# Whole expert groups in three fp32r products instead of full float32 ones: a mixture-of-experts kernel on one Trainium2 core

## The chip, the core and the metric

The kernel runs on one core of one Trainium2 chip. The metric is the device time of one execution in microseconds, as the median of repeated runs. TensorE (PE) multiplies, VectorE (DVE), ScalarE (ACT) and GpSimd (POOL) do the rest, and SyncE (SP) issues the loads of weights.

## The reference, cut to what matters

Two layers over 256 latent tokens (and 256 context tokens that only the first mixer reads), width 1024. Each layer is a token mixer followed by a mixture of experts; a final norm ends it. What matters here is the mixture:

```
def swiglu(x, w_gu, w_down):
    g, u = jnp.split(x @ w_gu, 2, axis=-1)
    return (jax.nn.silu(g) * u) @ w_down
...
    def expert_block(args):
        tok, w, e = args
        return swiglu(x_pad[tok], w_gu[e], w_down[e]) * w[:, None]
...
    return routed + swiglu(xn, ws_gu, ws_down)
```

There are 64 experts of inner width 256; each token goes to 8 of them, and one shared expert sees all. An expert's weights are three tiles of 1 MB: two of gate and up (128 x 2048 floats each, four chunks of 512 columns), one of down.

## The kernel before

**Experts by rank.** The router's counts sort the experts. The five largest, two natural ones and the shared one are *dense*: they run over all 256 tokens, with weights split into a high part (a cast to fp32r, `wh`) and a low part (the rest, `wl`), three products a step (`mm3`). The other experts get 32 to 128 slots each. Four units of 32 slots make a *group* of 128 rows; two groups make a batch, 11 batches a layer. In batches 0, 5 and 9 the first group (groups 0, 10 and 18) holds one expert with all 128 slots; the other groups hold two to four experts side by side, each on its own columns of the PE array. All groups multiply in full float32.

**A batch.** `first(i)`: gate and up of group i in two halves of four steps (`gate_up`), the transposed slot matrix (`slot_side`), and for i = 0 the scatter of the batch before. `second(i)`: transpose of the inner values (`flip`, tile `ht`), half of the next batch's `gather` of tokens (tile `xg`), then `down`, which writes `Y` with ScalarE (high part) and VectorE (low part). At a batch's start GpSimd builds the slot matrix `S` of the next batch. Ahead of batch 0 stands a branch, `overflow`, that all engines pass.

**Order.** Every engine runs its instructions in the recorded order. A planner at build time (`Stream`, `until`, `COST`) guesses when each load lands and puts steps of dense experts (`up`) where a group's tiles would not be there yet. Loads go through a ring of twelve 1 MB tiles (`wr`, `wx`); SP issues one as soon as a tile is free.

**The splitter.** `splitter(tmp, tiles, eng, bufs)` makes high and low parts of one 512-column chunk at a time, two chunks ahead of the one asked for, out of one pool of `wh` and `wl` buffers that all splitters share:

```
            while len(out) < min(q + 3, last or 4 * len(tiles)):
...
                S.copy(out=hi, in_=t)
                eng(i, c).tensor_tensor(out=lo, in0=t, in1=hi.bitcast(F32), op=OP.subtract)
```

`lower` gives even chunks to GpSimd, odd ones to VectorE. In the functions below, L309 is the matmul helper, L566 and L567 the two parts of a chunk, L1407 the build of S, L1473 and L1475 the copies of gathered tokens, L1535 the copy of `ht`, L1548 and L1549 the two parts of Y.

Of the kernel before, what the change touches and what calls it, by code (L numbers as in the profile page):

```python
# [10 lines left out]
F32 = mybir.dt.float32  # L11
# [83 lines left out]
RK, GROUPS = make_plan()  # L95
NG = len(GROUPS)


# [133 lines left out]
ORDER = 4.0  # L232
COST = dict(step=1.46, down2=2.95, half=3.6, side=0.6, scatter=4.0, flip=0.25, gather=2.0, down=3.6)

# [69 lines left out]
def _body(nc, tc, a, pp, rp, ps, ps1, dr):  # L304
# [846 lines left out]
    def moe(l, tail):  # L1151
      rsb = bank()
      with tc.tile_pool(name=f"e{l}", bufs=1) as mp, tc.tile_pool(name=f"e{l}t", bufs=2) as tp:
# [36 lines left out]
        def over_all(ns, gate=None, eng=None, early=None):  # L1190

            wq = splitter(tp, ns, eng or lower, 5)
            if early is not None:
# [34 lines left out]
        def all_down(f, n):  # L1228

            f, at = f  # L1230
            wq = splitter(tp, [n], lower, 5)

# [229 lines left out]
        def gather(b, half):  # L1462
# [3 lines left out]
            for d2 in range(2 * half, 2 * half + 2):  # L1466
# [4 lines left out]
                o = xg[:, 2 * d2:2 * d2 + 2, :].rearrange("p a s -> p (a s)")  # L1471
                if d2 % 2:
                    S.copy(out=o, in_=p)  # L1473
                else:
                    V.tensor_copy(out=o, in_=p)  # L1475
# [30 lines left out]
        gu = {}  # L1506

        def gate_up(g, ks=range(8)):
            xg = xgs[g // 2]
            b0 = (g % 2) * P  # L1510
# [4 lines left out]
            for k in ks:  # L1515
                for q, j, o, wd in rr:
                    mm(p[o:o + wd, :], xg[:, k, b0 + o:b0 + o + wd], st.tile(wt[q][k // 4])[:, 512 * (k % 4):512 * (k % 4) + 512], k == 0, k == 7)
                if k % 4 == 3:
                    for q in sorted({u[0] for u in GROUPS[g]}):
                        if last_use[q] == g:  # L1520
                            st.free(wt[q][k // 4])
            if 7 not in ks:
                return
            h = tp.tile([P, 256], F32, name="h", bufs=2)
# [4 lines left out]
        def flip(g):  # L1529
            h = hts[g]  # L1530
            p = bank()
            for k in range(2):
                PE.transpose(p[:, k * P:(k + 1) * P], h[:, k * P:(k + 1) * P], ident)  # L1533
            o = tp.tile([P, 2, P], F32, name="ht", bufs=2)
            S.copy(out=o, in_=p[:, :256].rearrange("p (k s) -> p k s", k=2))  # L1535
            hts[g] = o

        def down(g):
# [3 lines left out]
            for c in range(2):  # L1542
                p = bank()
                for k in range(2):
                    for q, j, o, wd in rr:
# [6 lines left out]
            for q in sorted({u[0] for u in GROUPS[g]}):  # L1552
                if last_use[q] == g:
                    st.free(wt[q][2])
# [35 lines left out]
        for b in range(NB):  # L1590
# [6 lines left out]
            def first(i):  # L1597
                g = 2 * b + i
                qs = sorted({u[0] for u in GROUPS[g]})
                for part in range(2):  # L1600
                    until([wt[q][part] for q in qs])
                    gate_up(g, range(4 * part, 4 * part + 4))
                    spend("half")
                slot_side(g)
# [5 lines left out]
            def second(i):  # L1610
# [6 lines left out]
                down(g)  # L1617
                spend("down")

            for step in (first, second) if b + 1 < NB else ():  # L1620
                for i in range(2):
                    step(i)
# [56 lines left out]
```

## Time and profile before

| | us |
|---|---|
| median of 3 runs | 1469.41 (1467.08 to 1471.1) |
| the profiled execution | 1469.6 |
| its span, first to last instruction | 1467.7 |
| TensorE busy (matmuls) | 1392.4, 95% of the span |
| VectorE, ScalarE, GpSimd busy | 753.6, 518.7, 331.8 |

The page gives busy shares over the whole span. The kernel has stages with different limits: the first mixer to about 250 us, mixture 0 to about 770 us, the second mixer to about 950 us, mixture 1 to the end. A busy share in a stage comes from the windows view, and what ends an engine's idle time from the waits and the timeline.

### The profile page before, as it was taken

Reading aid. Unit: us, or ns where it says so; the run is one execution under the profiler, and the core shown is the slowest. Engines: PE = TensorE matmul, PEld = TensorE weight load, DVE = VectorE, ACT = ScalarE, POOL = GpSimd, SP = SyncE. Lnnn points to the kernel's source line nnn. Section 1 sums busy time; section 2 is a strip of 40 time slices with the busy share of each in tenths; the row PEclk is TensorE's granted clock in tenths of the full one; section 3 lists DMA queues with packets and bytes.
Section 4 is the critical chain, followed back from the end, with each engine's and each line's share of the span. In section 5 each row is a group of like instructions: output and inputs, shape, how many; then the busy total and the mean of one; then the engine's idle time right before and its main releaser. Section 6 shows DMA issues by size and latency. Waiting matters only on the chain. (4 is left out here: it accounts for less than half of the span.)

```text
span 1467.7 us, 27203 instructions
## 1 busy us (share of the span) xinstructions
PE 1392.4 (95%) x10752; PEld 973.3 (66%) x10752; DVE 753.6 (51%) x1375; ACT 518.7 (35%) x874; POOL 331.8 (23%) x415
## 2 busy tenths in 40 slices
PE   6999997899999999999999999899999999999997
PEld 4677776656566575666657899775656666566664
DVE  6789997524343333334346786542334334343534
ACT  4777882422122222222225445432212222212222
POOL 1300044421222112312001451431212212111210
PEclk9999999899999999999999999999999999999999
DMA  9876694589989999999999744369999999999994
GB/s 376 321 276 245 245 375 186 222 351 409 412 362 405 420 420 420 420 418 421 420 418 388 289 163 173 116 251 412 394 389 372 421 421 421 420 419 420 420 420 182
DMA packets 77443, 514.85 MB, mean 351 GB/s; under 512 B 9856, under 2 KB 10240, under 8 KB 17024
## 3 DMA queue, kind: packets, MB, share of 16 engines
q1 hardware_dynamic: 74720, 508.91, 85.3%
q10 hardware_dynamic: 2592, 4.16, 0.9%
q8 instruction: 86, 1.41, 0.4%
q14 instruction: 45, 0.37, 0.1%
HBM read 511.99 MB, written 1.05 MB: 350 GB/s over the span
## 5 line engine op out<-in xcount | busy, mean ns | idle before, releaser
L309 PE MATMUL b<-wr,xg 128*32 128x512 f32 (+2 forms) x1464 | 306.5, 600 | 4.6 <-DMA wr<-in_m_gu 2.9
L567 POOL TENSOR_TENSOR wl<-wr,wh 128x512 fp32r<-128x512 f32 (+1 forms) x82 | 121.2, 1492 | 704.5 <-ACT wh L566 654.5
L309 PE MATMUL b<-wx,xg 128*32 128x512 f32 (+2 forms) x744 | 234.3, 598 | 1.7 <-SPq L1430 1.4
L566 ACT CAST wh<-wr 128x512 fp32r<-128x512 f32 (+1 forms) x230 | 147.4, 682 | 84.5 <-PE b L309 44.8
L567 DVE TENSOR_TENSOR wl<-wr,wh 128x512 fp32r<-128x512 f32 (+1 forms) x148 | 145.4, 1010 | 57.6 <-ACT wh L566 57.4
L309 PEld LDWEIGHTS b<-wr,xg 128*32 128x32 f32 (+2 forms) x1464 | 83.9, 118 | 134.9 <-issue 119.5
L1159 DVE SCALAR_TENSOR_TENSOR xT<-b,mod,xT 128x256 f32<-128x256 f32 x304 | 130.0, 478 | 60.5 <-PE b L309 54.5
L309 PE MATMUL s<-hh,wh 128*128 128x256 f32 x512 | 152.3, 297 | 1.1 <-ACT wh L566 1.1
L309 PE MATMUL s<-hh,wl 128*128 128x256 f32 x512 | 145.5, 284 | 3.7 <-DVE wl L567 1.9
L1526 DVE TENSOR_TENSOR h<-h,b 128x256 f32<-128x256 f32 x44 | 18.5, 420 | 252.4 <-ACT h L1525 252.4
L309 PE MATMUL s<-hl,wh 128*128 128x256 f32 x512 | 144.7, 283 | 0.0
L309 PE MATMUL b<-wr,ht 128*32 128x512 f32 (+2 forms) x712 | 141.9, 596 | 1.5 <-ACT ht L1535 1.5
L1549 DVE SCALAR_TENSOR_TENSOR Y<-b,gt,Y 128x512 fp32r<-128x512 f32 x88 | 65.8, 750 | 150.8 <-ACT Y L1548 150.8
L1525 ACT ACTIVATE h<-b 128x256 f32<-128x256 f32 x44 | 16.9, 384 | 351.0 <-PE b L309 351.0
L309 PEld LDWEIGHTS s<-hh,wh 128*128 128x128 f32 x512 | 98.2, 192 | 28.7 <-issue 25.3
L309 PE MATMUL b<-wx,ht 128*32 128x512 f32 (+2 forms) x392 | 109.1, 595 | 0.5 <-ACT ht L1535 0.5
L1548 ACT ACTIVATE Y<-b,gt 128x512 fp32r<-128x512 f32 x88 | 60.3, 687 | 135.8 <-PE b L309 129.5
L309 PEld LDWEIGHTS s<-hh,wl 128*128 128x128 f32 x512 | 98.1, 192 | 4.8 <-DVE wl L567 2.5
L1407 POOL TENSOR_SCALAR S<-cst,agq 128x32 fp32r<-128x32 f32 (+3 forms) x208 | 83.2, 429 | 72.2 <-PE b L309 54.5
L567 POOL TENSOR_TENSOR wl<-wx,wh 128x512 fp32r<-128x512 f32 (+1 forms) x36 | 53.6, 1506 | 199.2 <-ACT wh L566 192.6
L309 PEld LDWEIGHTS s<-hl,wh 128*128 128x128 f32 x512 | 98.3, 192 | 0.4
L309 PE MATMUL b<-S,xt 128*128 128x256 f32 x704 | 94.5, 287 | 0.0
(283 smaller groups left out, 2744.3 us busy)
## 6 DMA issues: line engine op xcount, KB each, us to landing
wr<-in_m_gu SPq DMA_DIRECT2D x167, 1024.0 KB, 12.7
wx<-in_m_gu SPq DMA_DIRECT2D x89, 1024.0 KB, 12.8
wr<-in_m_dn SPq DMA_DIRECT2D x80, 1024.0 KB, 11.1
wx<-in_m_dn SPq DMA_DIRECT2D x42, 1024.0 KB, 11.4
wr<-in_ada_w SPq DMA_DIRECT2D x32, 1024.0 KB, 9.1
wr<-in_a_in SPq DMA_DIRECT2D x10, 1024.0 KB, 8.1
wr<-in_ada SPq DMA_DIRECT2D x8, 1024.0 KB, 12.2
wr<-in_b_out SPq DMA_DIRECT2D x6, 1024.0 KB, 7.2
```

Of the source, the lines that this page charges most:

```text
L309: PE.matmul(out, lhsT, rhs, start=start, stop=stop, skip_group_check=True)
L566: S.copy(out=hi, in_=t)
L567: eng(i, c).tensor_tensor(out=lo, in0=t, in1=hi.bitcast(F32), op=OP.subtract)
L1159: V.scalar_tensor_tensor(out=xT[:, d, :], in0=y, scalar=mod[:, l, 5, d:d + 1], in1=xT[:, d, :], op0=OP.mult, op1=OP.add)
L1407: (G if b else V).tensor_scalar(out=s[:, tt, i * P + o:i * P + o + wd], in0=C["iota1"][:, j:j + wd], scalar1=agq[:, tt, q:q + 1], scalar2= ...
L1525: S.activation(out=h, in_=p[:, :256], func=AF.Silu)
L1526: V.tensor_tensor(out=h, in0=h, in1=p[:, 256:], op=OP.mult)
L1548: S.activation(out=hi, in_=p, func=AF.Copy, scale=gts[g])
L1549: V.scalar_tensor_tensor(out=y[:, 1, 512 * c:512 * c + 512], in0=p, scalar=gts[g], in1=hi.bitcast(F32), op0=OP.mult, op1=OP.subtract)
```

## The change

For the three groups a layer that hold one expert alone (`WHOLE`), gate, up and down run as three fp32r products a step on high and low parts, instead of one full float32 product. The gathered tokens of such a group are written as two parts (`xh`, `xl`) straight out of `gather`, the inner values as two parts (`h4`) out of `flip`, and the weights go through a splitter of their own: `begin` opens it, and asks for the first two chunks if the planner thinks that the tile has landed; for gate and up that is at the start of the batch, for down in `flip`. All splitters' pools have four buffers instead of five, and the planner's cost of a half of gate and up, and of down, is 2.8 instead of 3.6 for these groups.

```diff
--- before.py
+++ after.py
@@ -94,6 +94,9 @@
 
 RK, GROUPS = make_plan()
 NG = len(GROUPS)
+
+WHOLE = [len({q for q, _ in g}) == 1 for g in GROUPS]
+assert not any(WHOLE[1::2])
 
 
 def batch_tiles():
@@ -230,7 +233,7 @@
 LOAD, LATE = 2.6, -0.3
 
 ORDER = 4.0
-COST = dict(step=1.46, down2=2.95, half=3.6, side=0.6, scatter=4.0, flip=0.25, gather=2.0, down=3.6)
+COST = dict(whole=2.8, step=1.46, down2=2.95, half=3.6, side=0.6, scatter=4.0, flip=0.25, gather=2.0, down=3.6)
 
 READY = 5.0
 
@@ -1189,7 +1192,7 @@
 
         def over_all(ns, gate=None, eng=None, early=None):
 
-            wq = splitter(tp, ns, eng or lower, 5)
+            wq = splitter(tp, ns, eng or lower, 4)
             if early is not None:
                 early.append(wq)
             p, out, at = [], [], []
@@ -1228,7 +1231,7 @@
         def all_down(f, n):
 
             f, at = f
-            wq = splitter(tp, [n], lower, 5)
+            wq = splitter(tp, [n], lower, 4)
 
             def step(c):
                 pb2 = [bank(), bank()]
@@ -1469,7 +1472,15 @@
                     for n in range(4):
                         mm(p[:, 256 * i:256 * i + 256], xt[:, n // 2, n % 2, (2 * d2 + i) * P:(2 * d2 + i + 1) * P], s[:, n % 2, :], n == 0, n == 3)
                 o = xg[:, 2 * d2:2 * d2 + 2, :].rearrange("p a s -> p (a s)")
-                if d2 % 2:
+                if WHOLE[2 * b]:
+                    if d2 == 0:
+                        xls[b] = [tp.tile([P, 8, P], F32R, name=n, bufs=1) for n in ("xh", "xl")]
+                    o, pv = xg[:, 2 * d2:2 * d2 + 2, :], p.rearrange("p (a s) -> p a s", a=2)
+                    hi, lo = (x[:, 2 * d2:2 * d2 + 2, :] for x in xls[b])
+                    S.copy(out=hi, in_=pv[:, :, :P])
+                    V.tensor_copy(out=o[:, :, P:], in_=pv[:, :, P:])
+                    V.tensor_tensor(out=lo, in0=pv[:, :, :P], in1=hi.bitcast(F32), op=OP.subtract)
+                elif d2 % 2:
                     S.copy(out=o, in_=p)
                 else:
                     V.tensor_copy(out=o, in_=p)
@@ -1505,7 +1516,33 @@
 
         gu = {}
 
+        xls, wsp = {}, {}
+
+        def there(n):
+            return st.arrival(n) <= st.now
+
+        def begin(g, part):
+
+            q = GROUPS[g][0][0]
+            if WHOLE[g] and (g, part) not in wsp:
+                ns = wt[q][:2] if part == 0 else wt[q][2:]
+                wsp[g, part] = splitter(tp, ns, lower, 4)
+                if there(ns[0]):
+                    wsp[g, part](-1)
+
         def gate_up(g, ks=range(8)):
+            if WHOLE[g]:
+                xh, xl = xls[g // 2]
+                if 0 in ks:
+                    gu[g] = bank()
+                    begin(g, 0)
+                t1 = wt[GROUPS[g][0][0]][1]
+                for k in ks:
+                    w_ = wsp[g, 0](k, None if k > 3 or there(t1) else 4)
+                    mm3(gu[g], xh[:, k, :], xl[:, k, :], *w_, k == 0, k == 7)
+                if 7 in ks:
+                    hidden(g, gu[g])
+                return
             xg = xgs[g // 2]
             b0 = (g % 2) * P
             if 0 in ks:
@@ -1519,8 +1556,10 @@
                     for q in sorted({u[0] for u in GROUPS[g]}):
                         if last_use[q] == g:
                             st.free(wt[q][k // 4])
-            if 7 not in ks:
-                return
+            if 7 in ks:
+                hidden(g, p)
+
+        def hidden(g, p):
             h = tp.tile([P, 256], F32, name="h", bufs=2)
             S.activation(out=h, in_=p[:, :256], func=AF.Silu)
             V.tensor_tensor(out=h, in0=h, in1=p[:, 256:], op=OP.mult)
@@ -1531,8 +1570,16 @@
             p = bank()
             for k in range(2):
                 PE.transpose(p[:, k * P:(k + 1) * P], h[:, k * P:(k + 1) * P], ident)
+            pv = p[:, :256].rearrange("p (k s) -> p k s", k=2)
+            if WHOLE[g]:
+                o = tp.tile([P, 2, 2, P], F32R, name="h4", bufs=1)
+                S.copy(out=o[:, 0], in_=pv)
+                V.tensor_tensor(out=o[:, 1], in0=pv, in1=o[:, 0].bitcast(F32), op=OP.subtract)
+                hts[g] = o
+                begin(g, 1)
+                return
             o = tp.tile([P, 2, P], F32, name="ht", bufs=2)
-            S.copy(out=o, in_=p[:, :256].rearrange("p (k s) -> p k s", k=2))
+            S.copy(out=o, in_=pv)
             hts[g] = o
 
         def down(g):
@@ -1541,7 +1588,10 @@
             y = tp.tile([P, 2, D], F32R, name="Y", bufs=2)
             for c in range(2):
                 p = bank()
-                for k in range(2):
+                if WHOLE[g]:
+                    for k in range(2):
+                        mm3(p, o_[:, 0, k], o_[:, 1, k], *wsp[g, 1](2 * c + k), k == 0, k == 1)
+                for k in () if WHOLE[g] else range(2):
                     for q, j, o, wd in rr:
                         mm(p[o:o + wd, :], o_[:, k, o:o + wd], st.tile(wt[q][2])[:, 1024 * c + 512 * k:1024 * c + 512 * k + 512], k == 0, k == 1)
                 hi = y[:, 0, 512 * c:512 * c + 512]
@@ -1550,7 +1600,7 @@
                                        op0=OP.mult, op1=OP.subtract)
             ys[g] = y
             for q in sorted({u[0] for u in GROUPS[g]}):
-                if last_use[q] == g:
+                if last_use[q] == g and not WHOLE[g]:
                     st.free(wt[q][2])
 
         def scatter(b, tl=None):
@@ -1600,7 +1650,7 @@
                 for part in range(2):
                     until([wt[q][part] for q in qs])
                     gate_up(g, range(4 * part, 4 * part + 4))
-                    spend("half")
+                    spend("whole" if WHOLE[g] else "half")
                 slot_side(g)
                 spend("side")
                 if i == 0 and b:
@@ -1615,8 +1665,9 @@
                     spend("gather")
                 until([wt[q][2] for q in sorted({u[0] for u in GROUPS[g]})])
                 down(g)
-                spend("down")
-
+                spend("whole" if WHOLE[g] else "down")
+
+            begin(2 * b, 0)
             for step in (first, second) if b + 1 < NB else ():
                 for i in range(2):
                     step(i)
```

What it does to the order is seen in two places. ScalarE at the seam between batch 4 and batch 5 of layer 0 (Y of group 9, then group 10), before, with what each instruction waits for in brackets (the engine whose counter it watches; DMAHW is a landing):

```order
L1548 ACTIVATE Y_5056<-b_5057,gt_4874 128x512 [waits DVE_49,PE_49]
L1548 ACTIVATE Y_5056<-b_5064,gt_4874 128x512 [waits PE_49]
L1535 COPY ht_5096<-b_5093 128x256 [waits PE_49]
L1473 COPY xg_5035<-b_5108 128x512 [waits PE_49]
L566 CAST wh_5118<-wx1_4083 128x512 [waits Pool_49]
L1548 ACTIVATE Y_5145<-b_5146,gt_5028 128x512 [waits DVE_49,PE_49]
L1548 ACTIVATE Y_5145<-b_5157,gt_5028 128x512 [waits PE_49]
L1525 ACTIVATE h_5207<-b_5194 128x256 [waits PE_49]
L566 CAST wh_5263<-wx0_4172 128x512 [waits DMAHW3_49,Activation_49]
```

and now:

```order
L1582 COPY ht_5260<-b_5257 128x256 [waits PE_49]
L1480 CAST xh_5203<-b_5262 128x256 [waits PE_49]
L1480 CAST xh_5203<-b_5274 128x256 [waits PE_49]
L569 CAST wh_5286<-wx2_4255 128x512 [waits Activation_49]
L1598 ACTIVATE Y_5313<-b_5314,gt_5186 128x512 [waits DVE_49,PE_49]
L1598 ACTIVATE Y_5313<-b_5325,gt_5186 128x512 [waits PE_49]
L569 CAST wh_5353<-wr2_5076 128x512 [waits DMAHW2_49,Pool_49]
L569 CAST wh_5357<-wr2_5076 128x512 [waits Activation_49]
L569 CAST wh_5362<-wr2_5076 128x512 [waits PE_49,Pool_49]
L569 CAST wh_5369<-wr2_5076 128x512 [waits DVE_49,PE_49]
L569 CAST wh_5384<-wr4_5087 128x512 [waits DMAHW3_49,PE_49,Pool_49]
L569 CAST wh_5388<-wr4_5087 128x512 [waits DVE_49,PE_49]
```

The casts of group 10's gate and up chunks (six of the eight are shown) now stand between the last Y copy of group 9 and the activation `h` of group 10; from the third on they also wait for TensorE, whose earlier chunks hold the buffers.

GpSimd at the start of batch 0 of layer 0, behind the branch (S of batch 1, then low parts `wl`), before:

```order
L1407 TENSOR_SCALAR S_2846<-cst_71,agq_2559 128x64 [waits DVE_49]
L1407 TENSOR_SCALAR S_2846<-cst_71,agq_2559 128x64 x5
L1407 TENSOR_SCALAR S_2846<-cst_71,agq_2559 128x32 x4
L567 TENSOR_TENSOR wl_2892<-wx0_1989,wh_2891 128x512 [waits PE_49,DMAHW7_49,Activation_49,Pool_49]
L567 TENSOR_TENSOR wl_2902<-wx0_1989,wh_2901 128x512 [waits PE_49,Activation_49]
```

and now:

```order
L1410 TENSOR_SCALAR S_2856<-cst_71,agq_2559 128x64 [waits DVE_49]
L1410 TENSOR_SCALAR S_2856<-cst_71,agq_2559 128x64 x5
L1410 TENSOR_SCALAR S_2856<-cst_71,agq_2559 128x32 x4
L570 TENSOR_TENSOR wl_2868<-wr2_2497,wh_2867 128x512 [waits DMAHW6_49,PE_49,Activation_49]
L570 TENSOR_TENSOR wl_2877<-wr2_2497,wh_2876 128x512 [waits PE_49,Activation_49]
L570 TENSOR_TENSOR wl_2902<-wr4_2508,wh_2901 128x512 [waits DMAHW7_49,Activation_49]
L570 TENSOR_TENSOR wl_2916<-wr4_2508,wh_2915 128x512 [waits Activation_49]
```

Four low parts of group 0's gate and up (even chunks of tiles wr2 and wr4) have come in behind the block of S and ahead of the dense expert's (wx0).

## Rows read from the trace of the kernel before

**Rows 1.** The profile's page: TensorE's line, the granted clock and the DMA share in 40 slices.

```profile
PE 1392.4 (95%) x10752; PEld 973.3 (66%) x10752; DVE 753.6 (51%) x1375; ACT 518.7 (35%) x874; POOL 331.8 (23%) x415
...
PEclk9999999899999999999999999999999999999999
DMA  9876694589989999999999744369999999999994
```

**Rows 2.** Windows of two MoE stretches: length, busy us by engine, clock, DMA share, GB/s.

```profile
440.00:540.00 100.00, 99.05 (x791) 62.67 (x789) 35.52 (x66) 22.88 (x43) 19.72 (x29) 1.00 1.00 414
...
640.00:764.00 124.00, 122.20 (x1007) 75.81 (x1009) 50.77 (x91) 28.66 (x53) 22.22 (x30) 1.00 1.01 420
```

**Rows 3.** Waits of TensorE, 300 to 765 us: total us, times, longest.

```profile
PE b L309 <- ACT wh L566: 5.5, 2, 2.7
PE b L309 <- DMA wr<-in_m_gu: 1.4, 1, 1.4
```

**Rows 4.** Timeline of TensorE: a mixer stretch, down of group 0, group 10.

```profile
164.20 0.62 PE L309 MATMUL b<-us,wh 128*128 128x512 f32 x2
...
164.88 0.62 PE L309 MATMUL b<-us,wh 128*128 128x512 f32 x2
...
313.37 2.16 PE L309 MATMUL b<-S,xt 128*128 128x256 f32 x16
315.37 3.60 PE L309 MATMUL b<-wr,ht 128*128 128x512 f32 x8
318.80 0.38 PE L1533 MATMUL b<-cst,h 128*128 128x128 f32 x2
...
511.29 7.13 PE L309 MATMUL b<-wr,xg 128*128 128x512 f32 x16
518.26 0.27 PE L309 MATMUL b<-aqt,identb 128*128 128x256 bf16 x1
```

**Rows 5.** Timeline of ScalarE, layer 0.

```profile
313.65 0.37 ACT L1535 COPY ht<-b 128x256 f32<-128x256 f32 x1 [0.19 <-PE b L1533]
315.57 0.59 ACT L1473 COPY xg<-b 128x512 f32<-128x512 f32 x1 [1.54 <-PE b L309]
...
511.48 0.69 ACT L1548 ACTIVATE Y<-b,gt 128x512 fp32r<-128x512 f32 x1 [1.08 <-PE b L309]
...
612.94 2.70 ACT L566 CAST wh<-wr 128x512 fp32r<-128x512 f32 x5
```

**Rows 6.** Timeline of TensorE where a dense expert's down begins.

```profile
613.61 0.38 PE L309 MATMUL b<-fh,wh 128*128 128x256 f32 x1 [2.74 <-ACT wh L566]
...
614.97 0.58 PE L309 MATMUL b<-fh,wl 128*128 128x256 f32 x1 [0.77 <-POOL wl L567]
```

**Rows 7.** Timeline of GpSimd: S of batch 1, two low parts.

```profile
281.89 3.85 POOL L1407 TENSOR_SCALAR S<-cst,agq 128x64 fp32r<-128x64 f32 x10 [8.78 <-DVE flag L1587]
...
613.64 2.97 POOL L567 TENSOR_TENSOR wl<-wr,wh 128x512 fp32r<-128x512 f32 x2 [18.73 <-ACT wh L566]
...
970.45 3.84 POOL L1407 TENSOR_SCALAR S<-cst,agq 128x64 fp32r<-128x64 f32 x10 [8.96 <-DVE flag L1587]
```

**Rows 8.** Timeline of TensorE at group 0 of both layers.

```profile
282.45 8.80 PE L309 MATMUL b<-wr,xg 128*128 128x512 f32 x16 [1.75 <-DVEq L1430]
291.09 0.27 PE L309 MATMUL b<-aqt,identb 128*128 128x256 bf16 x1
...
970.91 3.67 PE L309 MATMUL b<-wx,xg 128*128 128x512 f32 x8 [1.36 <-SPq L1430]
...
977.85 0.27 PE L309 MATMUL b<-aqt,identb 128*128 128x256 bf16 x1
```

**Rows 9.** One window (columns as in group 2).

```profile
610.00:620.00 10.00, 6.49 (x40) 5.50 (x42) 6.44 (x9) 5.06 (x9) 4.69 (x4) 0.83 1.01 421
```

**Rows 10.** Timeline of VectorE at the same dense expert.

```profile
613.07 0.69 DVE L1221 TENSOR_TENSOR fl<-hf,fh 128x512 fp32r<-128x512 f32 x1 [0.68 <-ACT fh L1220]
614.11 3.04 DVE L567 TENSOR_TENSOR wl<-wr,wh 128x512 fp32r<-128x512 f32 x2 [0.35 <-ACT wh L566]
```

## The prediction

> **What bounds the kernel now.** I read the page first: TensorE (PE) is busy 95% of the span, at the full granted clock nearly throughout, and the DMA row is full in both MoE stages [rows 1]. Two resources at their limit in one stretch is the puzzle of this case: a faster TensorE is worth nothing if the loads set the pace. The windows show it sharper: from 440 to 540 us and from 640 to 764 us TensorE is busy 99 of 100 and 122 of 124 us, while the DMA engines carry 414 and 420 GB/s at a share of 1.00 [rows 2]. Which of the two ends last is told by the waits: in the MoE stage of layer 0 (300 to 765 us) TensorE's matmuls waited for a landing once, for 1.4 us; most of its few other waits were for ScalarE's casts [rows 3]. So loads land before they are wanted, and whatever TensorE does longer in this stage moves the end of the layer. The profiled execution took 1469.6 us around a span of 1467.7 us, and the median of the three runs is 1469.41 us; the sum below starts from 1469.6.
>
> **What the change removes.** Three groups of a layer are whole (0, 10 and 18), six in all. Gate and up of one are 8 full float32 products: 511.29 to the next instruction at 518.26, or 0.87 us a step; down is 4 of them, 315.37 to 318.80. Three fp32r products of 128x512 take 0.68 us in the first mixer (164.20 to 164.88) [rows 4]. A step saves 0.19 us, a group 12 x 0.19 = 2.3 us, all six 13.8 us. That is everything the change can give.
>
> **What it adds ahead of gate and up.** The weights are now cast (ScalarE), and their low part is subtracted (GpSimd for even chunks, VectorE for odd ones), before the second product of a step can start. Chunk 0 is asked for only when the previous batch's down has been recorded, so on ScalarE its cast stands behind the last Y copy of that down, as the order shows. That copy starts 0.19 us after TensorE has gone on to group 10 (511.48) and takes 0.69 us [rows 5]. From the start of a first cast (612.94 [rows 5]) to the first product took 0.67 us, and from there to the first product with a low part 1.36 us (613.61 and 614.97 [rows 6]). So the second product starts 0.19 + 0.69 + 0.67 + 1.36 = 2.91 us after TensorE is free, where it could start at 0.23 (a third of 0.68): 2.7 us of wait in groups 10 and 18, where the plan puts no other work in between. Nothing covers it.
> Group 0 starts behind the branch of the overflow test. There GpSimd first builds S of batch 1, from 281.89 to 285.74 in layer 0 and from 970.45 to 974.29 in layer 1 [rows 7], and the low part of chunk 0 is behind it in program order: its second product comes 1.36 us later, at 287.1 and 975.65, where group 0 started at 282.45 and 970.91 [rows 8]. That is some 4.5 us of wait.
>
> **What it adds inside gate and up.** For groups 0 and 18 all four buffers are free, and the pace is GpSimd's: two low parts in 2.97 us [rows 7], one in 1.49 us for two steps of together 1.36 us: 3 x 0.13 = 0.4 us. Group 10 is different. The pool goes from five buffers to four, and when group 10 starts, a paused dense expert still holds two of them with chunks not yet multiplied. In the built program chunk 2 takes the buffer of chunk 0, chunk 3 that of chunk 1, and so on, so that a cast waits until TensorE has ended the chunk two before it. Counted from a second product at t: the third at t + 0.23 with its end 0.39 later, the cast from t + 0.66 with the reaction, the first product of the next but one at t + 1.33, its second at t + 2.69. Two steps take 2.69 instead of 1.36 us, three times: 4.0 us.
> Sums for gate and up. Group 10: 2.7 + 4.0 - 1.5 saved = 5.1 us (second product at 514.2, end at 523.4 against 518.3). Group 18: 2.7 + 0.4 - 1.5 = 1.5 us. Group 0: from its second product 3 x 1.49 + 1.13 = 5.6 us to the end, so 292.7 against 291.09 in layer 0 (1.6 us) and 981.2 against 977.85 in layer 1 (3.4 us); layer 0's is smaller since its 8.6 us before are longer than 8 x 0.87.
>
> **Down.** The first two chunks are asked for in the transpose step, with a piece of gather (313.37 to 315.37) as cover [rows 4]. The cast starts where the copy of ht ends, at 314.02 [rows 5], so the second product comes at 316.05 instead of 315.60. Chunks 2 and 3 reuse the buffers of 0 and 1 in groups 0 and 10: cast about 316.75, end about 319.9 against 318.80, 1.1 us. In group 18 other buffers are free, but the cast stands behind the copy of xg (315.57 + 0.59): end 319.3, 0.5 us. Together 2.7 us a layer.
> The splits of the gathered tokens and of h (a copy and a subtraction more a bank) lie beside TensorE work, with ScalarE 23% and VectorE 36 to 41% busy [rows 2]: I take nothing; uncovered they cost a copy of 0.37 to 0.59 us [rows 5] in each of six groups, 3 us. For the dense experts four buffers still leave a chunk three steps of 12 products between release and use, some 4 us against the 2.0 of cast and low part: nothing.
>
> **The clock.** The stop that ends at 613.61 and its sequel (2.74 + 0.77 us idle [rows 6]) were followed by a granted clock of 0.83 over the 10 us from 610 to 620 [rows 9]: 1.7 us lost. The new stops are as long. Four a layer could fall to it, or none: 0 to 13.6 us. I take two in all, 3.4 us, near the low end, since the clock row shows few falls [rows 1].
>
> **Sum.** Layer 0: 1.6 + 5.1 + 1.5 + 2.7 = 10.9; layer 1: 3.4 + 5.1 + 1.5 + 2.7 = 12.7; clock 3.4; less 2 us of waits for landings that a later TensorE no longer has [rows 3]. That is 25 us: 1469.6 + 25 = 1494.6, so **1495 us**. The planner's changed costs move dense steps ahead of groups; their number stays.
>
> **A rule against the change.** VectorE and GpSimd now make low parts at once in every whole group. The rows: two took 3.04 us on VectorE [rows 10] beside the two of 2.97 us on GpSimd [rows 7], four from 613.64 to 617.15, so 1.75 us a pair. The Trainium skill (SBUF — State Buffer, section "SBUF: two separate sides") says that the two engines share a port pair under an exclusive lock, which a VectorE instruction with two SBUF inputs and a GpSimd one hold for their whole length; the rows agree in so far as either is slower than alone. If they strictly take turns, the sum rises to that of a rival below.
>
> **Rivals.**
> - *The loads absorb it* (about 1470). If a layer's end hung on its last landing, some microseconds of TensorE delay would vanish. For: full DMA engines [rows 2]. Against: TensorE hardly waits for landings [rows 3]. Chance 0.06.
> - *The casts run ahead and the gain comes through* (faster). Were the first casts done before the last Y copy, and buffers free, 13.8 us less some 4 us for group 0 would leave 1460. It decides at 0.23 us: the low part must be there that soon after TensorE is free, and by the rows it comes at 2.9. Chance 0.06.
> - *Low parts take turns.* VectorE's subtraction of this size takes 0.69 us undisturbed (613.07 [rows 10]); with GpSimd's 1.49 that is 2.18 us a pair, and (2.18 - 1.49) x 3 in the four groups 0 and 18 are 8 us more: 1503. Chance 0.14.
> - *Stop and go holds the clock at its lower level* (1.2 GHz) through groups 0 and 10: 1.7 us a stop for the remaining six stops and a little inside them, 12 us more: 1507. Chance 0.14.
> - *Half of it*: group 10 finds buffers after all or dense steps slip in between (8 us less), and the clock never falls (3 us less): 1484. Chance 0.10.
> The forecast itself, 1488 to 1500, has 0.50.
>
> **How the numbers follow.** The range goes from 1480 (the half case with a little to spare) to 1509 (the clock case); below it lie the first two rivals and some of the half case, above it some of the clock case, together 2 in 10. A difference of 0.3% (4.4 us) is about what a measurement of this kernel can tell from none. Faster 0.06, same 0.07 (the absorbing loads, and a little of the half case), slower 0.87.
>
> **What would show it.** In the changed kernel's profile: TensorE waiting about 2.7 us in front of groups 10 and 18 and over 4 us in front of group 0, ended by a low part on GpSimd; the 24 products of group 10 spread over some 12 us from the end of the previous down, against 8.5 us for group 18; each MoE stage longer by 11 to 14 us, the mixers unchanged; waits for landings still small. I am wrong if the stops are there and the span does not grow (then the loads set the pace), or if the low parts are ready when TensorE comes.

## The result and the profile after

The changed kernel takes 1533.43 us (median of 4 runs, 1530.58 to 1535.09), the kernel before 1470.26 in the same comparison: a ratio of 1.044 (95% interval 1.042 to 1.046). The forecast was 1495 us, range 1480 to 1509. The direction was right, the size not: 25 us slower expected, 63 measured. In the runs below, one execution of e3 (4753 us) and one of e6 (2319 us) ran in a far slower state; the ratios leave them out. The profiled execution has a span of 1533.1 us against 1467.7.

The page of the changed kernel (columns as in [rows 1]):

```profile
PE 1413.8 (92%) x10824; PEld 1006.2 (66%) x10824; DVE 810.6 (53%) x1453; ACT 563.1 (37%) x958; POOL 381.3 (25%) x451
...
PEclk9999998899999999999999999889999999999999
```

TensorE is busy 21 us longer although each of 72 steps is shorter: it runs more at the lower clock. The windows say where (columns as in [rows 2]):

```profile
275.00:525.00 250.00, 225.70 (x1735) 152.15 (x1734) 95.73 (x171) 61.41 (x114) 63.08 (x84) 0.93 0.86 347
525.00:800.00 275.00, 261.05 (x2130) 167.60 (x2129) 123.05 (x221) 78.66 (x147) 63.29 (x83) 0.98 0.97 401
...
440.00:540.00 100.00, 93.48 (x722) 61.99 (x716) 38.59 (x72) 24.39 (x46) 22.96 (x31) 0.97 0.94 380
```

From 440 to 540 us TensorE was busy 99 us with full DMA engines [rows 2]; now it is busy 93.5 and the DMA share falls to 0.94. So TensorE is late by itself. Its waits in this layer, 275 to 805 us, which answer to [rows 3] (us in total, times, longest):

```profile
PE b L312 <- ACT wh L569: 15.8, 9, 3.2
PE b L312 <- POOL wl L570: 15.1, 18, 4.3
PE s L312 <- ACT wh L569: 1.9, 2, 1.4
PE s L312 <- POOL wl L570: 1.7, 2, 0.9
PE b L312 <- DVE over L1633: 1.7, 1, 1.7
```

No landing is among them; 34.5 us are waits for casts and low parts. The timeline of TensorE at groups 0 and 10 answers to [rows 4, 8], and its third part is a place of which the prediction did not speak, the first down step of a dense expert:

```profile
282.15 0.18 PE L312 MATMUL b<-onesf,over 64*1 64x1 f32 x2 [1.67 <-DVE over L1633]
284.46 0.54 PE L312 MATMUL b<-wh,xh 128*128 128x512 f32 x1 [2.13 <-ACT wh L569]
289.28 0.80 PE L312 MATMUL b<-wl,xh 128*128 128x512 f32 x1 [4.29 <-POOL wl L570]
297.31 0.28 PE L312 MATMUL b<-aqt,identb 128*128 128x256 bf16 x1
...
538.65 0.49 PE L312 MATMUL b<-wh,xh 128*128 128x512 f32 x1 [1.37 <-ACT wh L569]
540.00 0.51 PE L312 MATMUL b<-wl,xh 128*128 128x512 f32 x1 [0.86 <-POOL wl L570]
542.85 0.80 PE L312 MATMUL b<-wl,xh 128*128 128x512 f32 x1 [0.56 <-POOL wl L570]
549.51 0.50 PE L312 MATMUL b<-wl,xh 128*128 128x512 f32 x1 [0.85 <-POOL wl L570]
550.77 0.28 PE L312 MATMUL b<-aqt,identb 128*128 128x256 bf16 x1
...
336.17 0.58 PE L312 MATMUL b<-fh,wh 128*128 128x256 f32 x1 [3.25 <-ACT wh L569]
```

The forecast stops in front of groups 0 and 10 are there. The last row is another kind, in front of a dense expert, whose code the change left alone but for a buffer. ScalarE says what that cast stood behind:

```profile
332.74 0.59 ACT L1219 ACTIVATE hf<-s 128x512 f32<-128x512 f32 x1
334.98 0.62 ACT L1223 CAST fh<-hf 128x512 fp32r<-128x512 f32 x1 [1.65 <-DVE hf L1222]
335.50 2.18 ACT L569 CAST wh<-wr 128x512 fp32r<-128x512 f32 x4
```

ScalarE closes one half (SiLU, then `fh`, which waits 1.65 us for VectorE's product), and only behind that casts the next half's first chunk. The experiments ask what brought these stops: the planner's costs, the buffers, or the whole groups' casts.

### The profile page after: what moved, and what is told of

Same layout as the page of the kernel before. It is cut to its first block, busy times and chain, and to the rows that moved or that the text cites. A ratio compares the mean times of both kernels' runs of the same rounds, so it can differ in the third digit from the quotient of the medians.

```text
span 1533.1 us, 27644 instructions
## 1 busy us (share of the span) xinstructions
PE 1413.8 (92%) x10824; PEld 1006.2 (66%) x10824; DVE 810.6 (53%) x1453; ACT 563.1 (37%) x958; POOL 381.3 (25%) x451
## 5 line engine op out<-in xcount | busy, mean ns | idle before, releaser
L312 PE MATMUL b<-wr,xg 128*32 128x512 f32 (+1 forms) x1368 | 261.2, 596 | 0.0
L570 DVE TENSOR_TENSOR wl<-wr,wh 128x512 fp32r<-128x512 f32 (+1 forms) x164 | 167.0, 1045 | 90.0 <-ACT wh L569 89.9
L569 ACT CAST wh<-wr 128x512 fp32r<-128x512 f32 (+1 forms) x250 | 159.3, 677 | 103.6 <-PE b L312 40.5
L312 PE MATMUL b<-wx,xg 128*32 128x512 f32 (+1 forms) x744 | 193.4, 597 | 0.0
L570 POOL TENSOR_TENSOR wl<-wx,wh 128x512 fp32r<-128x512 f32 (+1 forms) x68 | 97.2, 1442 | 228.8 <-ACT wh L569 214.3
L312 PE MATMUL b<-wr,ht 128*32 128x512 f32 (+1 forms) x760 | 138.3, 596 | 2.0 <-ACT ht L1582 2.0
L312 PEld LDWEIGHTS b<-wr,xg 128*32 128x32 f32 (+1 forms) x1368 | 67.8, 114 | 99.8 <-issue 93.9
L569 ACT CAST wh<-wx 128x512 fp32r<-128x512 f32 (+1 forms) x150 | 90.3, 636 | 93.4 <-PE b L312 37.8
L570 DVE TENSOR_TENSOR wl<-wx,wh 128x512 fp32r<-128x512 f32 (+1 forms) x82 | 76.5, 954 | 59.9 <-ACT wh L569 59.6
L312 PE MATMUL b<-fh,wh 128*128 128x256 f32 x256 | 81.6, 319 | 21.9 <-ACT wh L569 21.9
```

Source lines behind the costliest of these rows:

```text
L312: PE.matmul(out, lhsT, rhs, start=start, stop=stop, skip_group_check=True)
```

## The experiments

The first three change one part of the change each; e4 gives the lost buffer back.

**e1, four buffers alone**, on the kernel before:

```diff
-            wq = splitter(tp, ns, eng or lower, 5)
+            wq = splitter(tp, ns, eng or lower, 4)
...
-            wq = splitter(tp, [n], lower, 5)
+            wq = splitter(tp, [n], lower, 4)
```

> The kernel before with one edit: the dense experts' casts share four buffers instead of five; arithmetic and order of steps as before. The open question is why dense experts now stop at their first steps (about 18 us of idle TensorE in layer 0 of the changed kernel against 7 before, most with a stretch at the lower clock behind it). Theory B (buffers: the first casts of an expert can't run ahead): 1490 to 1510 us, with 2 to 4 more stops a layer of 1 to 3 us in front of a dense expert. Theory O (order: the planner's new cost opens an expert directly in front of its first step): 1470 to 1473 us, stops as before. If it takes both, 1470 to 1476.

1470.34 us, ratio 1.0007 (0.9988 to 1.0026). Alone, the loss of the fifth buffer costs nothing.

**e2, the planner's costs alone**, on the kernel before:

```diff
-                    spend("half")
+                    spend("whole" if WHOLE[g] else "half")
...
-                spend("down")
+                spend("whole" if WHOLE[g] else "down")
```

> The kernel before with one edit: the planner counts 2.8 instead of 3.6 us for the halves and downs of whole groups, so the dense steps stand between the groups exactly as in the changed kernel; arithmetic (full float32 products) and five buffers as before. Theory O: the dense experts' stops appear here too, 1490 to 1510 us, with lower-clock stretches behind them. Theory B: 1468 to 1473 us. If it takes both (or the split path of whole groups holding engines and buffers), 1468 to 1476.

1496.81 us, ratio 1.0178 (1.0144 to 1.0213): 27 us slower, with the arithmetic untouched. Waits of TensorE in layer 0, 275 to 805 us:

```profile
PE b L311 <- ACT wh L568: 11.3, 7, 3.3
PE b L311 <- POOL wl L569: 5.1, 6, 0.9
PE s L311 <- ACT wh L568: 1.9, 2, 1.4
PE s L311 <- POOL wl L569: 1.8, 2, 0.9
```

The same rows of the kernel before hold 6.2, 1.3, 0.5 and 0.9 us: 8.9 against 20.1, 11 us more in this layer. Layer 1 has its share: TensorE is idle 24.6 us there (980 to 1480 us) against 14.8 in the kernel before (960 to 1455).

**e3, the old order** in the changed kernel:

```diff
-COST = dict(whole=2.8, step=1.46, ...
+COST = dict(whole=3.6, step=1.46, ...
```

> The changed kernel with one edit: the planner counts 3.6 us for whole groups as before, so the dense steps stand as in the kernel before; split arithmetic and four buffers stay. Theory O: the dense stops and half-clock stretches of layer 0 go, 1495 to 1510 us, near the forecast, since only the whole groups' own stops stay. Theory B: 1525 to 1535. If it takes both: 1495 to 1510 too, and e2 near 1470 tells this from theory O.

1527.7 us, ratio 1.038 (1.033 to 1.043). Only 6 to 9 us come back (by the medians or by the ratios), not 27: the two costs do not add. Against e1, which has the same order and four buffers, the whole groups cost 56 us here. In this order group 18 takes turns as group 10 does: TensorE stops for a low part every 2.84 us, and gate and up take 11.7 us against 8.3 in the changed kernel. The reading is that a dense expert, left half done in front of the group, holds buffers.

```profile
707.34 0.50 PE L312 MATMUL b<-wl,xh 128*128 128x512 f32 x1 [0.84 <-POOL wl L570]
710.18 0.51 PE L312 MATMUL b<-wl,xh 128*128 128x512 f32 x1 [0.84 <-POOL wl L570]
```

**e4, five buffers** in the changed kernel, with room from two names:

```diff
-                o = tp.tile([P, 2, 2, P], F32R, name="h4", bufs=1)
+                o = tp.tile([P, 512], F32R, name="hf", bufs=1).rearrange("p (x k s) -> p x k s", x=2, k=2)
...
-                wsp[g, part] = splitter(tp, ns, lower, 4)
+                wsp[g, part] = splitter(tp, ns, lower, 5)
```

(`sel` and `mk` move into the name `h`, and both dense splitters go to five as well.)

> The changed kernel with five buffers again for the dense experts' and whole groups' casts; room for them comes from keeping the split h in the name of a dense expert's temporary and two routing tables in the names of the groups' h (no arithmetic changes); the order is the changed kernel's. Theory B: dense stops go and group 10's turns get shorter, 1490 to 1510 us. Theory O: only group 10's turns shorten (up to 4 us a layer), 1524 to 1532. If it takes both: 1495 to 1512, with e1 near 1470.

1527.07 us, ratio 1.0386 (1.0349 to 1.0422). Theory B falls: TensorE still waits 15.7 us for casts in layer 0 (15.8 in the changed kernel), so the dense stops stay, and it is mainly the turns of group 10 that shorten.

**e5, group 0 first.**

```diff
+        take_batch(0)
+        begin(0, 0)
         gather(0, 0)
...
                     gate_up(g, range(4 * part, 4 * part + 4))
                     spend("whole" if WHOLE[g] else "half")
+                if g == 0:
+                    build_s(1)
```

(`cape` and `over` also move ahead of the gather.)

> The changed kernel with three moves for group 0 and nothing else: the test value of the overflow branch is computed ahead of the gather, the first two chunks of group 0 are cast ahead of the gather too, and GpSimd builds S of batch 1 behind gate and up of group 0. Theory Q (queues: a stop comes from a cast or low part standing behind other work on its engine): the waits of 1.7, 2.1 and 4.3 us in front of and in group 0 go in both layers, 16 us less, and some or all of the 5 us that the lower clock costs there in each layer: 1507 to 1519 us. Theory R (rate: casts and low parts are too slow for three products a step, whatever stands ahead): the stops come back two chunks later, 1526 to 1534 us.

1531.15 us, ratio 1.0425 (1.0398 to 1.0452): a miss for theory Q. TensorE and GpSimd:

```profile
284.42 0.77 PE L312 MATMUL b<-wh,xh 128*128 128x512 f32 x1 [4.52 <-SPq L1433]
284.98 0.63 PE L312 MATMUL b<-wl,xh 128*128 128x512 f32 x1
291.48 0.28 PE L312 MATMUL b<-aqt,identb 128*128 128x256 bf16 x1
296.68 0.58 PE L312 MATMUL s<-hh,wl 128*128 128x256 f32 x1 [3.56 <-POOL wl L570]
```
```profile
290.14 5.26 POOL L1410 TENSOR_SCALAR S<-cst,agq 128x64 fp32r<-128x64 f32 x10
```

Group 0 is cured (7.1 us instead of 12.9), but TensorE starts it no earlier, now for the branch itself (SP's sequencer), and the stop of GpSimd's S build has moved to the next low part behind it, a dense expert's: 3.56 us. Theory R's range holds the time, but not by its mechanism, a stop two chunks later in the same group.

**e6, first casts of groups 10 and 18 ahead of the last down:**

```diff
+                if i and b + 1 < NB:
+                    take_batch(b + 1)
+                    begin(2 * b + 2, 0, True)
                 down(g)
```

> The changed kernel with one move: the first two chunks of groups 10 and 18 are cast ahead of the last down of the batch before, instead of behind it. Theory Q: the wait of 1.37 and one of 0.85 us in front of each of these four groups go, group 10's turns stay: 1522 to 1528 us. Theory R: 1530 to 1535, the time is spent in later chunks of the same group.

1530.62 us, ratio 1.0414 (1.0381 to 1.0446). The wait of 1.37 us goes, but the build of S (535.02 to 539.29 at group 10, 710.54 to 715.67 at group 18) now stands between the group's first and second low part on GpSimd, and TensorE waits 1.34 and 3.23 us there. The stop moved again.

**e7, openings ahead.** e2 with a dense half's first casts recorded one step earlier (gate and up) or two (down):

```diff
-            ups.append((lambda: wq(-1), ns[0], 0.0, None))
+            ups.insert(max(len(ups) - 1, 0), (lambda: wq(-1), ns[0], 0.0, None))
...
-            ups.append((lambda: wq(-1), n, 0.0, None))
+            ups.insert(max(len(ups) - 2, 0), (lambda: wq(-1), n, 0.0, None))
```

> The kernel before with the changed kernel's order (the run of 1496.8 us), and one move: the opening of a dense expert's half (its first two casts) stands one step earlier for the next gate and up, two steps earlier for a down, so that it is ahead of the closing work (SiLU, product, split of the inner values) of the half before on ScalarE. Theory Q: the 7 stops of 1.2 to 3.3 us with 0.85 us behind each go in front of dense halves: 1472 to 1482 us. Theory R, or a cause in the loads: 1490 to 1498 us.

1445.28 us, ratio 0.9846 (0.982 to 0.9871): 51 us below e2, and faster than the kernel before. The stops are gone, and more than theory Q gave. From 305 to 735 us:

```profile
305.00:735.00 430.00, 429.02 (x3494) 275.84 (x3490) 176.73 (x325) 105.35 (x196) 91.59 (x134) 1.00 1.01 419
```

TensorE is busy 429 of 430 us at the full clock. So the kernel before had such stops too, with the lower clock behind them; [rows 6] shows one.

**e9, the same in the old order** (e7's diff on the kernel before):

> The kernel before with the earlier openings of dense halves alone: full float32 products, five buffers, the old planner costs. If the planner's order costs something only through the openings (theory Q), the two orders are now equal: 1440 to 1450 us, like the run of the new order with early openings (1445.3). If the old order is better in itself: 1418 to 1432, the 27 us of the first comparison again.

1449.82 us, ratio 0.986 (0.9844 to 0.9877). With openings ahead the two orders are the same within what can be told; one stop of 2.22 us a layer is left in the old one. The order had no cost of its own that these runs can tell; it decided how many openings stood bare.

**e10, the same in the changed kernel** (e7's diff):

> The changed kernel with the earlier openings of dense halves alone (four buffers, its own order, its own late casts for whole groups). Against the run with full products, the new order and early openings (1445.3), it holds only what the whole groups cost. By the difference of the changed kernel and the new order alone (1533.4 less 1496.8): 1445 plus 37, so 1477 to 1487 us. If the dense openings and the whole groups hold each other up: 1460 to 1472, or over 1492.

1499.71 us, ratio 1.0205 (1.0188 to 1.0222), 54 us above e7 and not 37. One group makes the difference. TensorE in group 0, ScalarE ahead of it and in it, TensorE in group 10, and the windows of both groups:

```profile
291.94 0.80 PE L312 MATMUL b<-wh,xh 128*128 128x512 f32 x1 [0.76 <-ACT wh L569]
...
294.59 0.80 PE L312 MATMUL b<-wh,xh 128*128 128x512 f32 x1 [0.71 <-ACT wh L569]
295.94 0.79 PE L312 MATMUL b<-wl,xh 128*128 128x512 f32 x1 [0.55 <-POOL wl L570]
```
```profile
275.14 0.62 ACT L569 CAST wh<-wx 128x512 fp32r<-128x512 f32 x1 [0.73 <-PE s L312]
...
291.27 0.62 ACT L569 CAST wh<-wr 128x512 fp32r<-128x512 f32 x1 [5.53 <-PE b L312]
293.92 0.62 ACT L569 CAST wh<-wr 128x512 fp32r<-128x512 f32 x1 [2.03 <-PE b L312]
```
```profile
529.57 0.50 PE L312 MATMUL b<-wl,xh 128*128 128x512 f32 x1 [0.86 <-POOL wl L570]
...
532.42 0.50 PE L312 MATMUL b<-wl,xh 128*128 128x512 f32 x1 [0.84 <-POOL wl L570]
...
535.26 0.50 PE L312 MATMUL b<-wl,xh 128*128 128x512 f32 x1 [0.85 <-POOL wl L570]
```
```profile
284.00:312.00 28.00, 16.00 (x27) 6.67 (x27) 2.77 (x4) 5.07 (x9) 8.85 (x14) 0.53 0.13 41
...
525.00:542.00 17.00, 12.04 (x67) 7.16 (x60) 8.25 (x11) 7.54 (x13) 6.37 (x5) 1.00 1.02 423
```

A dense half is now opened ahead of group 0 (its two casts from `wx`, the second at 275.14) and not multiplied until the group is done. From its second chunk on every cast of group 0 waits for TensorE to end the step before (5.53 and 2.03 us), one chunk at a time, where group 10 takes two: with the lower clock that makes 26 us for 24 products, 12 to 13 us more than in the changed kernel, in either layer. That the dense half's chunks hold the buffers is the reading; the rows show the wait. Groups 10 and 18 and the downs cost about what they cost in the changed kernel, and group 10 shows its turns at the full clock: 2.84 us for two steps.

**e8 and e11, all ahead.** e8 is e4, e5, e6 and e7 together; e11 moves S behind gate and up of every whole group, and takes the low part of the weights in a step's third product:

```diff
-            if 0 < b < NB - 1:
+            if b + 1 < NB and not WHOLE[2 * b]:
                 build_s(b + 1)
...
-                if g == 0:
-                    build_s(1)
+                if WHOLE[g] and b + 1 < NB:
+                    build_s(b + 1)
...
+        mm(out, xh, wh, start, False)
+        mm(out, xl, wh, False, False)
+        mm(out, xh, wl, False, stop)
```

> The changed kernel with all moves at once: five buffers, group 0's three moves, first casts of groups 10 and 18 ahead of the down, openings of dense halves earlier; the changed kernel's planner costs. Theory Q: nearly all of the stops go, and what is left is the 13.8 us saved against some turns in group 10: 1456 to 1478 us, with the kernel before at 1470. Theory R: above 1495 us.

> The run with all moves (1460.0) with two more: GpSimd builds the next S behind gate and up of a whole group instead of in front of it, and the product with the low part of the weights is third in a step, not second. Theory Q: the stops of 2.1 and 3.6 us in groups 10 and 18 and the lower clock behind them go, 10 to 17 us less: 1443 to 1450 us. If the stops move to the next low part behind the S build: 1455 to 1461.

e8: 1459.98 us, ratio 0.994 (0.9917 to 0.9963). e11: 1447.64, ratio 0.985 (0.9834 to 0.9867). Both as theory Q has it. But e11 is no faster than e7 (1445.28), which has full products. Group 10 in e11, GpSimd, VectorE and TensorE:

```profile
506.87 4.70 POOL L576 TENSOR_TENSOR wl<-wr,wh 128x512 fp32r<-128x512 f32 x3 [3.43 <-PE b L312]
```
```profile
507.34 3.06 DVE L576 TENSOR_TENSOR wl<-wr,wh 128x512 fp32r<-128x512 f32 x2 [0.28 <-ACT wh L575]
```
```profile
505.40 0.50 PE L312 MATMUL b<-wh,xh 128*128 128x512 f32 x1
510.25 0.40 PE L312 MATMUL b<-wh,xh 128*128 128x512 f32 x1
511.96 0.39 PE L312 MATMUL b<-wh,xh 128*128 128x512 f32 x1
512.66 0.28 PE L312 MATMUL b<-aqt,identb 128*128 128x256 bf16 x1
```

Two steps take 1.71 us (510.25 to 511.96), as long as two full float32 steps (2 x 0.87 [rows 4]): the gain is gone, though no wait in the group is longer than 0.63 us. A low part takes 1.57 us on GpSimd (4.70 for three) beside 1.53 on VectorE (3.06 for two).

**e12, only groups 10 and 18 split**, in e11:

```diff
-WHOLE = [len({q for q, _ in g}) == 1 for g in GROUPS]
+WHOLE = [len({q for q, _ in g}) == 1 and i > 0 for i, g in enumerate(GROUPS)]
```

> The run e11 with group 0 back on full float32 products, so only groups 10 and 18 of each layer are split. If group 0's stops behind the branch cost more than its 2.3 us saving in each layer, this is the faster one: 1434 to 1444 us. If not, 1446 to 1454. A run below 1445.3 beats all full-product versions so far.

1455.38 us, ratio 0.9905 (0.9889 to 0.9922), above both ranges. Group 0's old cost also brings back part of the old order, and in layer 0 a dense down stops for 2.22 us at 604 us. So the run does not say what group 0 is worth alone.

**e13 and e14, low parts of whole groups on VectorE alone**, in the changed kernel and in e11:

```diff
-                wsp[g, part] = splitter(tp, ns, lower, 4)
+                wsp[g, part] = splitter(tp, ns, lambda i, c: V, 4)
```

> The changed kernel with one edit: all low parts of whole groups' weights are made by VectorE, none by GpSimd; order, four buffers and late casts stay. Theory G (GpSimd's queue and pace are the larger part of the whole groups' cost): the wait of 4.3 us in group 0 goes in both layers, a turn in group 10 shortens by GpSimd's 1.27 less VectorE's 0.69 us, and part of the lower clock in and behind group 0 goes: 1512 to 1524 us. Theory T (buffers taken in turns and stops at the lower clock keep the cost whatever engine subtracts): 1526 to 1534 us. Under both the dense halves' own stops stay.

> The run e11 (1447.6 us) with the low parts of whole groups on VectorE alone. There group 10 still takes 7.1 us for its 24 products, as in the kernel before, though nothing stands ahead of it: GpSimd's three low parts in 4.70 us beside VectorE's make two steps last 1.71 us. Theory G: with VectorE alone at 0.69 us a low part the group takes 5.6 to 6.2 us, and the six groups give 6 to 9 us: 1438 to 1442 us, faster than every run so far. Theory T, or VectorE too loaded with the copies of the previous down: 1445 to 1452 us.

e13: 1516.53 us, ratio 1.0314 (1.0286 to 1.0341), 17 us below the changed kernel by one line, inside theory G's range; TensorE's waits for GpSimd's low parts in layer 0 fall from 15.1 to this:

```profile
PE b L312 <- POOL wl L570: 5.3, 7, 0.9
```

e14: 1442.34, ratio 0.9817 (0.9787 to 0.9847). Group 10 in e14, VectorE and TensorE:

```profile
505.67 3.79 DVE L576 TENSOR_TENSOR wl<-wr,wh 128x512 fp32r<-128x512 f32 x6
```
```profile
504.09 0.50 PE L312 MATMUL b<-wh,xh 128*128 128x512 f32 x1
...
510.20 0.28 PE L312 MATMUL b<-aqt,identb 128*128 128x256 bf16 x1
```

The group takes 6.11 us against 7.26 in e11 and 6.97 before [rows 4]: theory G holds for the group, while the time is 0.3 us above its range and its interval overlaps e11's. e14 and e7 both beat the kernel before by some 25 us and the changed one by some 90; between them (ratios 0.982 and 0.985, intervals overlapping) the measurement can't tell. So of the 13.8 us that the three products were to save, no gain is shown even once everything else stands right: e7 has the 25 us with full products. Part of it goes in group 0, which takes 8.75 us in e14 (granted clock 0.66 from 282 to 292 us) against 6.95 in e7 (1.00).

## Why the prediction was wrong

**The failed step** is "The planner's changed costs move dense steps ahead of groups; their number stays", a term of nothing. It measured 27 us (e2). The number of steps does stay; what changes is which openings have a group's products between them and their first use, to cover the first casts. Where none stands there, the cast waits on ScalarE behind the closing work of the half before, a copy of gathered tokens or a Y copy, and TensorE behind it: 1.19 to 3.25 us, then up to 0.85 for the low part. The prediction's own [rows 6] showed such a stop, and I used it only as a price for whole groups. That the openings are the cause is shown: moved ahead, they make both orders equal (e7, e9). The 27 us is the order's price with full products. With the old order put back into the changed kernel only 6 to 9 us return (e3), so the forecast would have been too low without this step as well: the price of the whole groups hangs on the order too, 37 us in the new one and 56 in the old.

**Whole groups**, the rest of the sum, were to cost 25 us. Against the same order without them (e2) they cost 1533.4 - 1496.8 = 36.6; the terms that were too small are above all the clock and group 0. By group, from the row at which TensorE came free to the slot matrix behind gate and up, the changed kernel less e2 (group 10: 538.65 less its 1.37 of wait to 550.77, 13.5 us, against 528.12 to 535.10 in e2, 7.0):

| us | forecast | measured, layers 0 and 1 |
|---|---|---|
| group 0, with the wait for `over` | 1.6 and 3.4 | 7.7 and 6.9 |
| group 10 | 5.1 | 6.5 and 6.5 |
| group 18 | 1.5 | 2.7 and 2.7 |
| three downs | 2.7 | 3.0 and 3.1 |

The forecast counted group 0 against the kernel before; so counted it is 6.0 and 8.5. The rows hold the lower clock inside the groups. In layer 0 they make 19.9 us, nearly all of what the layer grew by (20.4, below).

The terms:

- *Start waits:* 2.7 us forecast for groups 10 and 18, 1.37 + 0.86 = 2.2 measured. Right.
- *Turns of group 10:* 2.69 us for two steps forecast, 2.84 measured at the full clock (e10). Right. In the changed kernel the same turns also met a clock of 0.66 from 540 to 550 us. With five buffers the group is 4.3 us shorter in layer 0 and 3.1 in layer 1 (e4). *Downs:* right.
- *Group 0:* its second product was forecast at 287.1 and came at 289.28. The splits of the gathered tokens, taken as nothing, hold VectorE up ahead of `over` (1.67 us of wait, 0.3 before), so the branch and the S build behind it start later, at 283.51 against 281.89 [rows 7]; the build takes 4.49 us instead of 3.85. Then the group runs partly at the lower clock (0.63 from 284 to 298 us).
- *Pace:* 1.49 us for two steps was too little. Side by side, low parts give 1.71 us (e11), which takes back the whole saving in a step; e14 shows 0.86 us of the 1.5 forecast for a gate and up once GpSimd is out.
- *The clock:* 3.4 us forecast for both layers, the term of this sum that was missed by most. In layer 0 the windows above give 250 x 0.07 + 275 x 0.02 = 23 us lost. That is some 13 us above the kernel before, whose two windows (275 to 500 us at 0.97, 500 to 770 at 0.99) lose 9.5, and above e2, whose windows (275 to 525 us at 0.97, 525 to 780 at 0.99) lose 10. In layer 1 the same count gives 5 us before (960 to 1455 us), 10 in e2 (980 to 1480) and 26 in the changed kernel (995 to 1520). So the order's cost is mostly waits, and the lower clock, 29 us in both layers over e2, comes mostly with the whole groups. By place, in windows of 10 us, layer 0 loses 10 us more at groups 0, 10 and 18 and 5 more behind the dense openings between 330 and 500 us.
- *The count for layer 0, changed kernel less e2:* TensorE idle 13.7 us more (38.2 against 24.5 in these windows), clock 13, products 6.9 less: 19.8. From the point at which TensorE is free for `over` to the end of the last down the layer takes 20.4 us more (280.48 to 797.0 against 282.26 to 778.4).
- *Landings:* they stayed out of the waits, and nothing shows that loads absorbed anything. The forecast was right that TensorE's delay moves the end.

**The rivals.** "Stop and go" was nearest in kind, with too low a price. "Low parts take turns" (8 us) is not borne out as priced: it took GpSimd's 1.49 us, which had been measured beside VectorE's low parts and so held waiting already. VectorE alone takes 0.63 us a low part (3.79 for six in e14), GpSimd 1.27; strictly in turn a pair would take 1.9 us, and the pace in e11 was 1.71. In group 10 of the changed kernel VectorE's, started beside GpSimd's, ends 0.54 us after it (550.00 against 549.46), little less than it takes alone:

```profile
548.19 1.27 POOL L570 TENSOR_TENSOR wl<-wr,wh 128x512 fp32r<-128x512 f32 x1 [2.06 <-ACT wh L569]
...
548.94 1.06 DVE L570 TENSOR_TENSOR wl<-wr,wh 128x512 fp32r<-128x512 f32 x1 [2.21 <-ACT wh L569]
```

The Trainium skill (SBUF — State Buffer, section "SBUF: two separate sides") has such instructions of the two engines hold a shared port pair under an exclusive lock, each for its whole length. These rows agree in the main, while the pace of 1.71 us is a little under strict turns.

What stays open: the split between waits and clock is a count and no experiment, since no run could hold the clock; why the whole groups cost 19 us more in the old order than in the new, of which group 18's turns are only a part; and what group 0 alone is worth (e12).

## What to carry to other kernels

A planner's cost is part of the program: before a change to it is priced at nothing, count the places where a fresh cast or load now stands directly in front of its first use, and look on the casting engine for what stands ahead of it. Work moved ahead in one queue delays whatever follows in that queue (the S build in e5 and e6), so follow the moved stop to its next consumer. And a step that is shortened from 0.87 to 0.68 us is worth nothing if its operands are made at 0.86 us a step.

## What the runs showed of the hardware

In e10 the 28 us from 284 to 312, nearly all of them group 0, ran at a granted clock of 0.53, so nearly all of it at 1.2 GHz, with TensorE busy 16 of 28 us and idle 0.55 to 0.76 us ahead of three in every six products. Group 10's turns in the same run, with stops of 0.85 us at every sixth product, stood at 1.00 over 17 us; the same turns in the changed kernel fell to 0.66 from 540 to 550 us. So stops of this size went with either level, and the runs don't show what decides. In e7, where TensorE hardly stops, the clock never falls from 305 to 735 us. The Trainium skill (TensorE: Matmul & The Clock Gate, section "HAM oscillation — how this bites in real kernels") describes a kernel whose pieces of work are shorter than the waits between them, and where each wait brings the lower clock back. Group 0 of e10 is like it in that the lower clock stayed, but its waits are shorter than the work between them, and no run here shows that the cause is the same.

VectorE's low part of a chunk takes 0.63 us in a row of six alone and 1.53 beside GpSimd's, and giving GpSimd half of the low parts was slower in a whole group than giving it none (e13, e14).
